# Hybrid conv, latent-attention and memory block: sums of the high and low parts of x, written by adding transfers instead of GpSimd

## The chip, the cores and the metric

The kernel runs on one core of one Trainium2 chip. A core has five engines that each work through their own list of instructions in order: TensorE (PE, matrix products), VectorE (DVE), ScalarE (ACT), GpSimd (POOL) and SyncE (SP, which here only issues transfers). They meet through semaphores. Transfers can be issued from SP, ScalarE and GpSimd, and are carried out by 16 DMA engines which all of them share. The metric is the time of one execution on the device in microseconds (us); the profile's times count from the start of its span.

## The reference

One layer of a streaming encoder, on 512 tokens of width 2048, in float32. The normalised input `h` goes through one wide input projection, whose columns feed three branches: a gated convolution, latent attention with 16 heads, and cross attention to 256 memory tokens. Each branch is gated, projected to 2048, weighted by a sigmoid gate, summed, and projected once more:

```python
h = rms_norm(x, norm_g[l])
proj = h @ w_in[l]
...
o_conv = (conv_y * jax.nn.silu(conv_z)) @ w_conv_out[l]
o_mla = (mla_y * jax.nn.silu(mla_z)) @ w_mla_out[l]
o_mem = (mem_y * jax.nn.silu(mem_z)) @ w_mem_out[l]
merged = sigmoid(g_conv) * o_conv + sigmoid(g_mla) * o_mla + sigmoid(g_mem) * o_mem
x = x + merged @ w_o[l]
```

## The kernel before

**Three products for one.** TensorE multiplies float32r operands. Each operand is split into a high part (ScalarE rounds it: `act.activation(hi, src, AF.Copy)`, L123) and a low part, the rest (VectorE: `src - hi`, L125), and a product is made of three matmuls, high x high, high x low and low x high (`mm3`, L154 to L156).

**The normalised input.** `h` is held transposed, as 16 tiles of 128 features x (high, low) x 512 tokens. Early on, SP writes them to a buffer in device memory, `hdram[k]` (shape 128 x 2 x 512, index 0 the high part, 1 the low part; L455), and reads them back after the attention (L693) into the tiles `xt[k]`: `blk` for k below 8, `hU` above.

**The planner.** From there on all the work of TensorE is a list of chunks, `plan`, and `drive()` writes the instructions of all engines chunk by chunk. For each chunk it writes, in this order: hooks that hang on this chunk number (`at[c]`, mostly loads of weights on SP), the combination of weights that a coming chunk needs (`pre`), the split of the weights of a chunk some numbers ahead (`prep`, ScalarE's high part `whi` and VectorE's low part `wlo`), small pieces that are due (`todo`, ordered by their due chunk), pieces that may run when there is room (`spare`), and then the matmuls of the chunk itself (`mm`). Nothing reorders an engine's list after that: SP's order is the written order for the whole kernel (`tc.manual_schedule`, L116), and that of the four others for this stage (L1481). A wait in such a list holds everything written behind it on the same engine.

**Two kinds of chunks.** Chunks 0 to 23 are plain: four blocks of 128 output columns, two blocks of 128 features, matmuls with 512 columns. Chunks 16 to 23 are the second half of the gate of the memory branch (`w_memz[1]`). The weights of a plain chunk are loaded by SP four chunks ahead (L852) into `raw`, a tile with four buffers. From chunk 24 on, the work comes in block groups (`block_group`), where a 2 x 2 block product is made with seven products in place of eight (`PRODUCTS`: P1, P7, P5, P6, P2, P4, P3, two chunks each, matmuls with 256 columns). The first group is the first of `w_conv`; it loads eight tiles of weights, w0 to w7 (L903), two each at chunks 21, 22, 23 and 24. Some products take sums or differences of these tiles: for P7, chunk 26 needs `s` = w0 - w2 and chunk 27 `s` = w1 - w3 (L968, VectorE), and the ones after that work in the same way in place (L973).

**The forms of x.** The block products also need sums and differences of the blocks of `h`. The tokens are halved, and feature tile p (0 to 7) is paired with tile p + 8. For each p, `x_forms(p)` has three pieces:

- `blocks` (L1212): a tile `eo` with the two whole values, high + low, of `xt[p]` and of `xt[p + 8]`. GpSimd adds them (L1215, L1216), 128 x 512 each. `eo` has the tag `r0` for even p and `r1` for odd p, each with one buffer; the tile for p + 2 takes the place of that for p.
- `sums` (L1219, with `sums_of`, L1015 to L1019): four VectorE operations make the differences and sums of the halves. L1015 reads both halves of `eo` first, L1019 reads it last.
- `parts_` (L1229): these are split into high and low parts, `f`, by ScalarE and VectorE (L123, L125).

A fourth piece, `place_t1`, splits one of the differences into the place of half of `xt[p]`.

`blocks` of p = 0 and 1 are written at chunk 15, that of p + 2 at chunk 16 + p, `sums` and `parts_` of p at chunk 17 + p (the planner gives these numbers from its own costs; pieces due at once, like `blocks`, come ahead of the spare ones, like `sums`). So `blocks` of p + 2 is written ahead of the `sums` of p that it must wait for, which are in another engine's list. The four `y` tiles that the memory gate is multiplied with (L1052, from `mydram`) are loaded at chunk 22, ahead of w2 and w3.

Of the kernel before, what the change touches and what calls it, by code (L numbers as in the profile page):

```python
# [22 lines left out]
ALU = mybir.AluOpType  # L23
# [49 lines left out]
def r32(ap):  # L73
    return ap.bitcast(F32)
# [21 lines left out]
def body(ctx, tc, a, out):  # L96
    nc = tc.nc
    act, vec, pool = nc.scalar, nc.vector, nc.gpsimd
# [177 lines left out]
    hdram = dram.tile([KB, P, 2, S], F32, name="hdram")  # L276
# [38 lines left out]
    for grp in range(4):  # L315
# [12 lines left out]
        if grp < 2:  # L328
# [12 lines left out]
            for f2 in range(2):  # L341
                b = bank("aux")
                for ff in range(2):
                    for i in range(2):
                        f = 2 * f2 + ff
                        nc.tensor.transpose(out=b[:, ff * M + i * P:ff * M + (i + 1) * P],
                                            in_=krow[i][:, f * P:(f + 1) * P], identity=ident)
# [336 lines left out]
    xt = {}  # L684
# [144 lines left out]
    def raw_b(dtype=F32):  # L829
        return psw.tile([P, KC, 512], dtype, tag="raw", name="raw", bufs=6)  # L830
# [170 lines left out]
    def operands(b0, b1, f):  # L1001
        return {"00": (b0[:, 0, :HS], b0[:, 1, :HS]), "T1": (b0[:, 0, HS:], b0[:, 1, HS:]),
                "10": (b1[:, 0, :HS], b1[:, 1, :HS]), "11": (b1[:, 0, HS:], b1[:, 1, HS:]),
                "T3": (f[:, 0, 0], f[:, 1, 0]), "T2": (f[:, 0, 1], f[:, 1, 1]), "T4": (f[:, 0, 2], f[:, 1, 2])}
# [3 lines left out]
    def f_tile(p):  # L1008
        return pf.tile([P, 2, 3, HS], F32R, name=f"f{p}")

    def sums_of(e, o, t1, then=lambda: None):

        t = pres.tile([P, S], F32, tag="u", name="t32")
        t4 = pres.tile([P, HS], F32, tag="v", name="t4", bufs=1)
        vec.tensor_tensor(out=t[:, :HS], in0=o[:, HS:], in1=e[:, HS:], op=ALU.subtract)  # L1015
        vec.tensor_tensor(out=t1, in0=e[:, HS:], in1=e[:, :HS], op=ALU.subtract)
        vec.tensor_tensor(out=t[:, HS:], in0=t[:, :HS], in1=e[:, :HS], op=ALU.add)
        then()
        vec.tensor_tensor(out=t4, in0=o[:, :HS], in1=t[:, HS:], op=ALU.subtract)  # L1019
        return t, t4  # L1020

    def split_sums(t, t4, f):
        split(pair(t), f[:, 0, :2], f[:, 1, :2])
        split(t4, f[:, 0, 2], f[:, 1, 2])
# [183 lines left out]
    def x_forms(p):  # L1208

        hold = {}  # L1210

        def blocks():  # L1212
            he, ho = xt[p], xt[p + 8]
            eo = pres.tile([P, 2, S], F32, tag=f"r{p % 2}", name="eo")
            pool.tensor_tensor(out=eo[:, 0], in0=r32(he[:, 0]), in1=r32(he[:, 1]), op=ALU.add)  # L1215
            pool.tensor_tensor(out=eo[:, 1], in0=r32(ho[:, 0]), in1=r32(ho[:, 1]), op=ALU.add)  # L1216
            hold["eo"] = eo

        def sums():  # L1219
            f = f_tile(p)  # L1220
            tx[p] = operands(xt[p], xt[p + 8], f)
            if p % 4 == 0:
                t1s["tile"] = raw_b()
            t1 = t1s["tile"].rearrange("p k n -> p (k n)")[:, (p % 4) * HS:(p % 4 + 1) * HS]
            t1s[p] = t1
            hold["t"] = sums_of(hold["eo"][:, 0], hold["eo"][:, 1], t1)
            hold["f"] = f

        def parts_():  # L1229
            split_sums(*hold["t"], hold["f"])  # L1230
        return blocks, sums, parts_
# [340 lines left out]
```

## Time and profile before

| what | value |
|---|---|
| time, median of 3 runs (lowest to highest) | 2219.71 us (2219.61 to 2223.3) |
| the profiled execution: its own time; its span | 2221.29 us; 2219.5 us |
| mean granted TensorE clock in it | 0.99 of full |
| GpSimd additions L1215, L1216 | 8 and 8, from 657.5 to 732.5 us |
| chunks 20 to 23 on TensorE | about 711.4 to 734.0 us |
| chunks 24 and 25; 26 and 27 | 734.1 to 739.8 us; 742.7 to 751.8 us |
| transfers over the span | 313.77 MB, mean 141 GB/s |

Rows of the profile read like this. In a timeline a row has the start, the duration, the engine (SPq stands for SP issuing transfers), the line, the operation, the tile written and the tiles read, shapes, and a count; rows of one kind that follow each other are merged, and the duration then runs from the first start to the last end. In brackets stands the engine's idle time ahead of the row and what ended it. In a list of waits a row has the waiting instruction, the one that released it, the total in us, how often, and the longest. In a list by line a row has min / median / max of the duration in ns, and the first and last start; a row on landing has the us from a transfer's issue to its landing, min / median / max, of the transfers that the row above it counts.

### The profile page before, as it was taken

To read this page: it belongs to the slowest core of one execution; us is meant where nothing else is said; L and a number is where in the kernel's file an instruction comes from. 1 tells how busy PE (TensorE), PEld (TensorE's weight loads), DVE (VectorE), ACT (ScalarE), POOL (GpSimd) and SP (SyncE) were. 2 spreads that over 40 slices of the span, in tenths; PEclk is the share of its full clock that TensorE was granted. 3 is DMA by queue.
4 is the path that set the end of the run, shared out by engine and by line. 5 is a ranking of instruction groups with operands and counts; after the bars stand their busy time and mean duration, and the time that the engine had idled before them with its cause. 6 is when DMAs were issued, how large, how long until landed. Compare 5 with 4: busy or idle time off the path is not lost.

```text
span 2219.5 us, 37222 instructions
## 1 busy us (share of the span) xinstructions
PE 2156.8 (97%) x15128; PEld 2019.9 (91%) x15128; DVE 1592.1 (72%) x2202; ACT 1025.3 (46%) x1547; POOL 193.6 (9%) x157
## 2 busy tenths in 40 slices
PE   7999999999999999999999999999999999997999
PEld 5788888888778899999999999999999899986999
DVE  7863777773336888787877777677776788867876
ACT  5532677764333444444444444444444444433343
POOL 7410311120012100000000000000000000012000
PEclk9999999999999999999999999999999999998999
DMA  7583212244225333333344434343245656465342
GB/s 258 155 258 101 85 58 70 69 148 147 76 76 189 115 105 100 138 102 115 124 174 171 134 115 153 115 152 134 97 145 170 244 205 200 157 237 190 115 171 86
DMA packets 110363, 313.77 MB, mean 141 GB/s; under 512 B 12656, under 2 KB 12912, under 8 KB 110192
## 3 DMA queue, kind: packets, MB, share of 16 engines
q1 hardware_dynamic: 87984, 271.20, 36.7%
q10 hardware_dynamic: 21888, 39.15, 4.7%
q8 instruction: 118, 1.93, 0.4%
q0 software_dynamic: 320, 1.05, 0.1%
q14 instruction: 53, 0.43, 0.1%
HBM read 263.12 MB, written 48.23 MB: 140 GB/s over the span
## 4 chain that ended last, share of the span: by engine, by line
PE 90%; DVE 5%; ACT 3%; issue 2%; POOL 1%; DMA 0%; SPq 0%; ACTq 0%; DVEq 0%; POOLq 0%
PE acc L154 17%; PE acc L155 17%; PE acc L156 16%; PE aux L155 12%; PE aux L156 12%; PE aux L154 12%; DVE wlo L148 1%; PE aux L205 1%; PE aux L661 1%; DVE wlo L125 1%; POOL xs L305 0%; DVE f L125 0%; DVE ml L127 0%; DVE hT L127 0%; PE aux L641 0%
## 5 line engine op out<-in xcount | busy, mean ns | idle before, releaser
L125 DVE TENSOR_TENSOR wlo<-raw,whi 128x1024 fp32r<-128x1024 f32 x440 | 539.8, 1228 | 375.9 <-ACT whi L123 375.6
L123 ACT ACTIVATE whi<-raw 128x1024 fp32r<-128x1024 f32 x440 | 465.9, 1060 | 710.0 <-PE acc L155 329.6
L973 DVE TENSOR_TENSOR raw<-raw 128x1024 f32<-128x1024 f32 x192 | 234.1, 1219 | 1.3
L154 PE MATMUL acc<-f,whi 128*128 128x256 f32 x768 | 216.8, 282 | 2.8 <-ACT whi L123 2.8
L156 PE MATMUL acc<-f,wlo 128*128 128x256 f32 x768 | 217.3, 283 | 1.6 <-DVE wlo L125 1.6
L155 PE MATMUL acc<-f,whi 128*128 128x256 f32 x768 | 216.9, 282 | 0.0
L156 PE MATMUL aux<-f,wlo 128*128 128x256 f32 x768 | 216.9, 282 | 0.0
L155 PE MATMUL aux<-f,whi 128*128 128x256 f32 x768 | 216.8, 282 | 0.0
L154 PE MATMUL aux<-f,whi 128*128 128x256 f32 x768 | 216.6, 282 | 0.0
L154 PE MATMUL acc<-blk,whi 128*128 128x256 f32 (+1 forms) x608 | 184.3, 303 | 7.0 <-ACT sq L1069 7.0
L148 DVE TENSOR_TENSOR wlo<-raw,whi 128x1024 fp32r<-128x1024 f32 (+3 forms) x97 | 117.8, 1216 | 96.6 <-ACT whi L147 95.4
L155 PE MATMUL acc<-blk,whi 128*128 128x256 f32 (+1 forms) x608 | 183.7, 302 | 0.0
L156 PE MATMUL acc<-blk,wlo 128*128 128x256 f32 (+1 forms) x608 | 183.2, 302 | 0.0
L155 PE MATMUL acc<-hU,whi 128*128 128x256 f32 (+1 forms) x608 | 182.1, 300 | 0.0
L154 PE MATMUL acc<-hU,whi 128*128 128x256 f32 (+1 forms) x608 | 182.1, 300 | 0.0
L156 PE MATMUL acc<-hU,wlo 128*128 128x256 f32 (+1 forms) x608 | 181.9, 300 | 0.0
L154 PE MATMUL aux<-blk,whi 128*128 128x256 f32 (+1 forms) x544 | 158.2, 291 | 14.4 <-ACT blk L123 12.9
L156 PE MATMUL aux<-blk,wlo 128*128 128x256 f32 (+1 forms) x544 | 158.3, 291 | 1.5 <-DVE wlo L125 1.5
L155 PE MATMUL aux<-blk,whi 128*128 128x256 f32 (+1 forms) x544 | 158.3, 291 | 0.4
L156 PE MATMUL aux<-hU,wlo 128*128 128x256 f32 (+1 forms) x544 | 156.9, 289 | 0.0
L155 PE MATMUL aux<-hU,whi 128*128 128x256 f32 (+1 forms) x544 | 156.9, 288 | 0.0
L154 PE MATMUL aux<-hU,whi 128*128 128x256 f32 (+1 forms) x544 | 156.7, 288 | 0.0
(354 smaller groups left out, 5642.0 us busy)
## 6 DMA issues: line engine op xcount, KB each, us to landing
raw<-in_w_conv SPq DMA_DIRECT2D x64, 512.0 KB, 4.4
raw<-in_w_mlaz SPq DMA_DIRECT2D x32, 512.0 KB, 5.1
raw<-in_w_gmem SPq DMA_DIRECT2D x32, 512.0 KB, 4.6
raw<-in_w_gconv SPq DMA_DIRECT2D x32, 512.0 KB, 4.8
raw<-in_w_gmla SPq DMA_DIRECT2D x32, 512.0 KB, 4.4
raw<-in_w_mla_out SPq DMA_DIRECT2D x32, 512.0 KB, 5.7
raw<-in_w_o SPq DMA_DIRECT2D x32, 512.0 KB, 6.3
raw<-in_w_mem_kv SPq DMA_DIRECT2D x31, 512.0 KB, 3.7
```

Source lines behind the costliest of these rows:

```text
L123: act.activation(hi, src, AF.Copy, scale=1.0 if g is None else g)
L125: vec.tensor_tensor(out=lo, in0=src, in1=r32(hi), op=ALU.subtract)
L148: vec.tensor_tensor(out=lo[:, cols], in0=raw[:, cols], in1=r32(hi[:, cols]), op=ALU.subtract)
L154: nc.tensor.matmul(o, lhsT=s[0], rhs=m[0], start=start, stop=False, skip_group_check=shared)
L155: nc.tensor.matmul(o, lhsT=s[0], rhs=m[1], start=False, stop=False, skip_group_check=shared)
L156: nc.tensor.matmul(o, lhsT=s[1], rhs=m[0], start=False, stop=stop, skip_group_check=shared)
L205: nc.tensor.transpose(out=b[:, i * P:(i + 1) * P], in_=s, identity=ident)
L661: nc.tensor.transpose(out=b[:, i * P:(i + 1) * P], in_=ps[i][:, j * P:(j + 1) * P], identity=ident)
L973: vec.tensor_tensor(out=w01, in0=i0, in1=i1, op=op)
```

## The change

GpSimd's additions in `blocks` are replaced by transfers. For each of the two halves of `eo`, SP loads the high part from `hdram` into `eo`, and GpSimd issues a second transfer that reads the low part from `hdram` and adds it to what stands in `eo` while writing. The second must wait until the first has landed. `xt` is no longer read here; `hdram` holds the same values. The place in the written order, the tags and the buffers stay as they were.

```diff
         def blocks():
-            he, ho = xt[p], xt[p + 8]
             eo = pres.tile([P, 2, S], F32, tag=f"r{p % 2}", name="eo")
-            pool.tensor_tensor(out=eo[:, 0], in0=r32(he[:, 0]), in1=r32(he[:, 1]), op=ALU.add)
-            pool.tensor_tensor(out=eo[:, 1], in0=r32(ho[:, 0]), in1=r32(ho[:, 1]), op=ALU.add)
+            for i in range(2):
+                nc.sync.dma_start(eo[:, i], hdram[p + 8 * i][:, 0])
+                nc.gpsimd.dma_start(out=eo[:, i], in_=hdram[p + 8 * i][:, 1], accum_op=ALU.add)
             hold["eo"] = eo
```

## The prediction

> **What bounds the kernel now.** I read the page first, then TensorE's waits around the change, then each engine in order of time there.
>
> ```profile
> PE 2156.8 (97%) x15128; PEld 2019.9 (91%) x15128; DVE 1592.1 (72%) x2202; ACT 1025.3 (46%) x1547; POOL 193.6 (9%) x157
> PE 90%; DVE 5%; ACT 3%; issue 2%; POOL 1%; DMA 0%; SPq 0%; ACTq 0%; DVEq 0%; POOLq 0%
> ...
> PE acc L154 <- ACT whi L123: 2.8, 1, 2.8
> PE acc L156 <- DVE wlo L125: 1.6, 1, 1.6
> ...
> 739.64 0.28 PE L156 MATMUL acc<-blk,wlo 128*128 128x256 f32 x1
> 742.72 0.38 PE L154 MATMUL acc<-f,whi 128*128 128x256 f32 x1 [2.81 <-ACT whi L123]
> 744.86 0.58 PE L156 MATMUL acc<-f,wlo 128*128 128x256 f32 x1 [1.64 <-DVE wlo L125]
> 751.78 0.28 PE L154 MATMUL acc<-blk,whi 128*128 128x256 f32 x1
> 744.00:746.00 2.00, 1.14 (x5) 1.14 (x6) 2.00 (x3) 0.84 (x1) 0.00 (x0) 0.62 0.63 225
> 746.00:748.00 2.00, 2.00 (x12) 2.00 (x12) 2.00 (x3) 1.34 (x2) 0.00 (x0) 0.52 0.00 0
> 748.00:750.00 2.00, 2.00 (x19) 2.00 (x18) 2.00 (x3) 1.13 (x2) 0.00 (x0) 1.00 0.00 0
> ```
>
> TensorE is the bound. Between 640 and 830 us it waits twice, both at the start of planner chunk 26 (product P7, first half). In the three windows of 2 us the granted clock stands behind the five engines' busy times: 0.62 and 0.52 after the stall, then 1.00 again. At full clock a 256-column matmul starts every 0.119 us (a chunk of 24 takes 2.9), so the 48 of chunks 26 and 27 need 5.7 us; they took from 739.76 to 751.78, 12.0. **The stall with its slow clock costs 6.3 us**, all that this region has to give.
>
> Why chunk 26 is late: VectorE.
>
> ```profile
> L125 DVE TENSOR_TENSOR f<-t,f 128x512 fp32r<-128x512 f32 (+1 forms) x12 | 19.1, 1627 | 1.4 <-ACT f L123 1.4
> ...
> 719.98 1.21 DVE L125 TENSOR_TENSOR wlo<-raw,whi 128x1024 fp32r<-128x1024 f32 x1
> 721.12 0.41 DVE L1015 TENSOR_TENSOR t<-eo 128x256 f32<-128x256 f32 x1
> 722.24 0.43 DVE L1019 TENSOR_TENSOR t<-eo,t 128x256 f32<-128x256 f32 x1
> 733.38 1.21 DVE L968 TENSOR_TENSOR s<-raw 128x1024 f32<-128x1024 f32 x1
> 734.52 1.21 DVE L125 TENSOR_TENSOR wlo<-raw,whi 128x1024 fp32r<-128x1024 f32 x1
> 737.44 1.03 DVE L125 TENSOR_TENSOR f<-t,f 128x512 fp32r<-128x512 f32 x2 [0.24 <-ACT f L123]
> 743.59 1.22 DVE L125 TENSOR_TENSOR wlo<-s,whi 128x1024 fp32r<-128x1024 f32 x1
> ...
> L1215 POOL TENSOR_TENSOR eo<-blk x8: 1283/1295/1337, 657.5 to 729.5; 128x512 f32<-128x512 f32 x8
> L1216 POOL TENSOR_TENSOR eo<-hU x8: 1299/1742/1750, 658.7 to 730.8; 128x512 f32<-128x512 f32 x8
> ```
>
> While GpSimd adds, the two `f` splits of a pair take 2 x 1.63 = 3.2 us; from 737.44, with GpSimd idle, they take 1.03. Six of the eight pairs pay 2.1 us. From 733.38 (the weight difference `s`, chunk 26's `pre`) to 744.81 (its low part) VectorE runs all but without a gap: 11.4 us.
>
> **Removed:** 16 GpSimd additions, some 24 us of POOL (8 x 1.30 + 8 x about 1.7), off TensorE's path, and with them 6 x 2.1 = 12.8 us of VectorE.
>
> **Added:** 16 plain loads of 256 KB on SP, and 16 accumulating loads on GpSimd, each behind the landing of its plain load. Each pair's loads also inherit the wait that the additions had: `eo` has one buffer for even pairs (`r0`), one for odd (`r1`), so pair p+2 waits until VectorE has done the sums of pair p (L1019). On GpSimd nothing was queued behind that wait. **On SP the weights are queued behind it.** SP keeps its written order, and the planner puts the work thus (a chunk is the line; SP's loads, then VectorE's forms):
>
> - chunk 16: weights of chunk 20, pair 2
> - chunk 17: weights of 21, pair 3; sums 0
> - chunk 18: weights of 22, pair 4; sums 1
> - chunk 19: weights of 23, pair 5; sums 2
> - chunk 20: pair 6; sums 3
> - chunk 21: w0, w1 of the first block group, pair 7; sums 4
> - chunk 22: four `y` tiles, w2, w3; low part of w0 (chunk 24), sums 5
> - chunk 23: w4, w5; `s` = w0 - w2 (chunk 26), low part of w1 (chunk 25), sums 6
> - chunk 24: sums 7, then chunk 26's low part
>
> So w0 sits behind pair 6, which waits for sums 4; and w2 sits behind pair 7, which waits for sums 5, which in VectorE's order stand behind w0's low part. Before, SP ran far ahead:
>
> ```profile
> 711.67 1.06 ACT L123 ACTIVATE whi<-raw 128x1024 fp32r<-128x1024 f32 x1 [0.52 <-ACT f L123]
> 717.27 1.06 ACT L123 ACTIVATE whi<-raw 128x1024 fp32r<-128x1024 f32 x1
> 723.69 1.04 ACT L123 ACTIVATE whi<-raw 128x1024 fp32r<-128x1024 f32 x1
> 703.18 6.34 SPq L903 DMA_DIRECT2D raw<-in_w_conv  x2
> 709.62 1.80 SPq L1052 DMA_DIRECT2D y<-mydram  x4
> 711.47 10.56 SPq L903 DMA_DIRECT2D raw<-in_w_conv  x6
> L852 SPq DMA_DIRECT2D raw<-in_w_memz x7: 327/328/333, 665.1 to 697.2; - x7
> DMA to landing us min/median/max: 3.6/3.7/4.6
> L903 SPq DMA_DIRECT2D raw<-in_w_conv x1: 430/430/430, 711.5 to 711.5; - x1
> DMA to landing us min/median/max: 7.5/7.5/7.5
> L903 SPq DMA_DIRECT2D raw<-in_w_conv x2: 430/430/430, 711.5 to 711.9; - x2
> DMA to landing us min/median/max: 7.5/7.9/8.3
> L903 SPq DMA_DIRECT2D raw<-in_w_conv x4: 328/430/1030, 711.5 to 715.2; - x4
> DMA to landing us min/median/max: 7.5/7.9/9.1
> ```
>
> The third and fourth rows from above are ScalarE's split of w0 and SP's issue of w0 and w1; the landing rows are w2 alone, w2 with w3, and w2 to w5. w0 went out at 703.2, w2 at 711.5, far ahead of their use at 723.7 and 733.4. The new chain, step by step:
>
> 1. Weights of chunks 21 to 23 now go out behind sums 0, 1, 2 plus two `eo` issues of 0.45 (the `y` row's 1.80 / 4). ScalarE splits chunk 22 at 711.67 and chunk 23 at 717.27, one chunk of TensorE apart (5.6); so chunk 21 at 706.07. Its low part starts at 707.1, sums 2 follow 1.14 later and take 1.55 (719.98, 721.12, 722.67 before): done at 709.8. Chunk 23's weights go out at 710.7 and land by 715.3 at the longest landing, 4.6. Hidden, with 2 us of room.
> 2. Low part of chunk 23 at 717.27 + 1.06 = 718.4 (before 719.98, with VectorE behind). Sums 4 follow and are done 2.7 later, at 721.1.
> 3. Pair 6 goes out at 721.1 and 721.55, w0 at 722.0. Landing 4.5 (the upper end, since 512 KB go ahead): 726.5, against 703.2 + 3.6 = 706.8 before.
> 4. ScalarE 1.06, low part 1.14, sums 5 1.55: 730.2. TensorE needs w0 at 734.0 (739.76 less two chunks of 2.9), so no stall yet.
> 5. Pair 7 from 730.2, four `y` from 731.1, w2 at 732.9, the seventh issue.
> 6. Landing of w2. The same burst without the pair ran before: first `y` at 709.62, w2 landed at 711.47 + 7.5 = 719.0, 9.35 later. A pair adds 512 KB ahead; in that burst neighbours of 512 KB landed about 1.25 apart (711.9 + 8.3 = 720.2 behind 719.0). So 730.2 + 9.35 + 1.25 = **740.8**. At the shortest landing, 3.6, it would be 736.5.
> 7. VectorE stands at `s` until then, and the low part of chunk 25 (734.52 before) stands behind it. TensorE finishes chunk 24 near 737 and waits for that low part until 743, then from about 746 to 752 for chunk 26. From `s` on VectorE's chain is the old one of 11.4 us, since GpSimd was idle through it before too (its last addition, 730.8 plus 1.7, ends at 732.5).
>
> **The sum:** chunk 26 moves by the shift of `s`, 740.8 - 733.4 = **+7.5 us** (+3.1 at the shortest landing). The old 6.3 us are not saved: the 11.4 us chain comes back whole, and the slow clock with it, as TensorE again idles some 5 us before. Behind it TensorE has no other wait up to 830, so the shift stays to the end. The 12.8 us that VectorE saves become waiting for w0 and w2. The profiled execution takes 2221.29 us (span 2219.5, 1.8 around it), inside the runs' 2219.61 to 2223.3; it would become 2228.8, and the median of 2219.71 becomes **2227.2**.
>
> **The unknown price: an accumulating load.** No row shows one. The nearest are GpSimd's plain stores of the same size, and a lone plain `eo` pair later:
>
> ```profile
> L678 POOL DMA_DIRECT2D ydram<-y x4: 539/544/753, 495.9 to 536.9; - x4
> DMA to landing us min/median/max: 2.3/2.5/5.0
> L1391 SPq DMA_DIRECT2D eo<-adram x2: 327/472/618, 1741.4 to 1741.8; - x2
> DMA to landing us min/median/max: 2.5/3.0/3.4
> ```
>
> Call it A, from GpSimd's issue to landing. One turn of a buffer is sums 1.55, second issue 0.48, landing 3.4, A: 5.4 + A, against two chunks of TensorE, 11.2. Up to A = 5.8 it hides behind the chunks; above, sums 4 come 2 x (A - 5.8) later after two turns, and so do w0, w2 and `s`. Lower end 2.3. Upper end 12: the crowded store's 5.0, twice for reading source and destination, and 2 for queueing beside the weights. I take 5, the crowded store, at which nothing is added; it costs +12.4 at the upper end.
>
> The Trainium skill (SBUF — State Buffer, "SBUF: two separate sides") says that GpSimd cannot write a transfer's descriptors while VectorE runs an operation that uses both port pairs. All VectorE rows quoted here are TENSOR_TENSOR, which the page ("Who interferes with whom") exempts, so by it A gains nothing; if they did lock, one 1.2 us operation for each of two issues would add up to 2.4 a turn, and A = 5 would then cost some 3 us over two turns. No row here can show it. The skill (DMA: Bandwidth & Descriptors, "Rules for kernel authors") also asks that an accumulating transfer wait for the earlier write's semaphore; without that wait the landing of 3.4 would leave the turn. No row shows either.
>
> **Rivals.**
>
> *Faster: VectorE's relief reaches TensorE.* Place: chunk 26. For it: `f` at 3.2 against 1.03 us beside GpSimd. Price: at most the 6.3 us, 2213.4. It decides from the point where w2 lands before 733.4; that needs it issued by 729.8, hence sums 5 done by 727.2, three us before step 4, or SP not held by the waits. Against: SP's four `y` loads at 709.62 went out only behind w1 (703.18 plus 6.34 ends at 709.5), so SP is in order.
>
> *Small loss.* The burst drains as a lone load does: +3.1, 2222.8. For it: 3.6 to 4.6 us landings of single loads. Against: 7.5 in the only like burst.
>
> *Slow accumulation paces the forms.* With A = 10: 7.5 + 8.4 = +15.9, 2235.6. For it: reading and rewriting the destination. Against: only 256 KB each, on a queue that is otherwise empty.
>
> *The change does not do what it says* (the transfers wait nowhere new, level): only if `eo` were free early; its buffers are not, L1019 reads them last.
>
> **How the numbers follow.** Three runs before spread over 0.17%, so 0.2%, 4.4 us, is what a measurement can tell. Forecast 55%, slow accumulation 22%, small loss 15%, faster 6%, level 2%. Slower takes the first two and a little of the small loss: 0.78. Same: the rest of that and level, 0.16. Faster 0.06. Range: from the small loss less the stretch of its steps, 2222, to A = 12, 7.5 + 12.4 = +19.9, 2239.6: it leaves out the faster case and the tails. The forecast alone spans +4.4 to +10, by the landing of w2 between 738 and 743.
>
> **What would show it.** Right: SP's `raw<-in_w_conv` w0 near 722 and w2 near 733, held by `DVE t L1019`; VectorE idle before `s` L968, released by a load; `f` near 1.0 us throughout; TensorE idle near 737 to 743 and again before chunk 26; that chunk at about 750. Wrong: w2 out before 729 (faster), sums 2 and 4 waiting for GpSimd's transfers (slow accumulation), or a stall of chunks 21 to 23, whose 2 us of room step 1 counts on. Wrong as a whole: TensorE's wait in 730 to 760 no longer than before.

## The result, and the profile after

The changed kernel takes 2233.4 us (median of 5, 2232.03 to 2245.25), the kernel before 2220.52 (median of 5, 2219.61 to 2223.3): a ratio of 1.0057, 95% interval 1.0029 to 1.0084, **slower by some 13 us**. 2227.2 had been predicted, 7.5 us above the runs known then, with a range of 2222.0 to 2239.6. The profiled execution took 2233.24 us with a span of 2231.4, 11.9 us longer than that of before.

Executions of most kernels here, the one before included (14 of 76 beside the experiments), fall into two groups some 10 us apart, for a reason that no trace here shows; where that shifts a median, the median of the lower group stands beside it.

Two clocks must be set against each other first. SP's `y` loads ahead of its first `eo` load (one row before, one after) show that the profiled execution after runs 2.0 us early when it comes to the changed stage:

```profile
672.48 1.80 SPq L1052 DMA_DIRECT2D y<-mydram  x4
```

```profile
670.50 1.80 SPq L1052 DMA_DIRECT2D y<-mydram  x4
```

So 2.0 is taken off each time that was predicted before it is compared. Some 1.5 of it stood before the change could act (VectorE's L1107 starts at 642.82 before and 641.33 after). The other 0.5 is a small gain of the change that the prediction did not have: before, the additions of pairs 0 and 1 run from 657.45 on, VectorE's L1116 beside them takes 1.81 us in place of 0.62, and eight of TensorE's matmuls (L205) that read what L1116 writes take 1.54 us in place of 1.03.

The page of after, busy time and share of each engine:

```profile
PE 2160.4 (97%) x15128; PEld 2022.4 (91%) x15128; DVE 1579.7 (71%) x2202; ACT 1025.5 (46%) x1547; POOL 185.1 (8%) x157
```

VectorE is busy 12.4 us less than before (1592.1), which is the relief that was forecast. TensorE around the block products: first every wait that it has between 640 and 850 us, in order of time, then two windows of 2 us with the granted clock (the third figure from the right).

```profile
733.56 0.39 PE L154 MATMUL acc<-blk,whi 128*128 128x256 f32 x1 [1.31 <-ACT whi L123]
734.82 0.39 PE L156 MATMUL acc<-blk,wlo 128*128 128x256 f32 x1 [0.76 <-DVE wlo L125]
...
747.76 0.58 PE L156 MATMUL acc<-blk,wlo 128*128 128x256 f32 x1 [8.34 <-DVE wlo L125]
...
754.69 0.39 PE L154 MATMUL acc<-f,whi 128*128 128x256 f32 x1 [1.86 <-ACT whi L123]
756.83 0.58 PE L156 MATMUL acc<-f,wlo 128*128 128x256 f32 x1 [1.64 <-DVE wlo L125]
```

```profile
748.00:750.00 2.00, 2.00 (x10) 2.00 (x11) 1.73 (x5) 1.26 (x4) 0.00 (x0) 0.50 1.08 338
...
758.00:760.00 2.00, 2.00 (x12) 2.00 (x11) 2.00 (x3) 1.38 (x2) 0.00 (x0) 0.54 0.00 0
```

The two waits of before (2.8 and 1.6 us, at chunk 26) are still there as 1.86 and 1.64. New is the wait of 8.34 us for the low part of chunk 25, and two small ones at chunk 24. Chunk 26 begins at 754.69 against 742.72, 12.0 us later. The clock stands at 0.50 after the long wait and once more near 0.54 after chunk 26's.

Why that low part was late. VectorE in order of time, SP likewise, and one row of SP's waits between 660 and 800 us:

```profile
696.21 0.43 DVE L1019 TENSOR_TENSOR t<-eo,t 128x256 f32<-128x256 f32 x1
...
708.97 0.42 DVE L1019 TENSOR_TENSOR t<-eo,t 128x256 f32<-128x256 f32 x1
...
723.27 0.42 DVE L1019 TENSOR_TENSOR t<-eo,t 128x256 f32<-128x256 f32 x1
723.93 1.03 DVE L125 TENSOR_TENSOR f<-t,f 128x512 fp32r<-128x512 f32 x2 [0.24 <-ACT f L123]
733.54 1.23 DVE L125 TENSOR_TENSOR wlo<-raw,whi 128x1024 fp32r<-128x1024 f32 x1 [7.91 <-ACT whi L123]
735.80 0.43 DVE L1019 TENSOR_TENSOR t<-eo,t 128x256 f32<-128x256 f32 x1
745.35 1.23 DVE L968 TENSOR_TENSOR s<-raw 128x1024 f32<-128x1024 f32 x1 [7.18 <-DMA raw<-in_w_conv]
755.56 1.22 DVE L125 TENSOR_TENSOR wlo<-s,whi 128x1024 fp32r<-128x1024 f32 x1
```

```profile
696.66 0.80 SPq L1215 DMA_DIRECT2D eo<-hdram  x2
709.42 1.25 SPq L1215 DMA_DIRECT2D eo<-hdram  x2
718.16 6.38 SPq L1215 DMA_DIRECT2D eo<-hdram  x4
724.64 0.89 SPq L903 DMA_DIRECT2D raw<-in_w_conv  x2
736.26 0.80 SPq L1215 DMA_DIRECT2D eo<-hdram  x2
737.11 1.85 SPq L1052 DMA_DIRECT2D y<-mydram  x4
739.06 47.41 SPq L903 DMA_DIRECT2D raw<-in_w_conv  x16
```

```profile
SPq L1215 <- DVE t L1019: 18.3, 6, 5.3
```

The first three rows are the ends of sums 0, 2 and 4. Sums 4 end at 723.69 (L1019 at 723.27 and 0.42); then SP issues pair 6, and w0 and w1 at 724.64. Sums 5 end at 736.23; SP issues pair 7 at 736.26, the four `y` tiles, and w2 at 739.06. VectorE idles 7.91 us until w0 is split and 7.18 until w2 has landed. This is the chain that was forecast, link by link, only later. `f` takes 1.03 us.

How long the loads took, in the list by line (a row on landing under the transfers that it counts: SP's plain loads of `eo`, GpSimd's adding ones, and w0 with w1; w0 is the 7.7):

```profile
L1215 SPq DMA_DIRECT2D eo<-hdram x16: 319/423/942, 678.8 to 736.6; - x16
DMA to landing us min/median/max: 2.8/5.0/7.0
L1216 POOL DMA_DIRECT2D eo<-hdram x16: 872/876/1883, 684.4 to 740.2; - x16
DMA to landing us min/median/max: 3.8/6.3/10.1
L903 SPq DMA_DIRECT2D raw<-in_w_conv x2: 385/397/409, 724.6 to 725.2; - x2
DMA to landing us min/median/max: 7.7/8.4/9.1
```

w2, issued at 739.06, landed 6.3 us later, when `s` starts.

### The profile page after: what moved, and what is told of

It reads as the page before. It is cut to its first block, busy times and chain, and to the rows that moved or that the text cites. A ratio compares the mean times of both kernels' runs of the same rounds, so it can differ in the third digit from the quotient of the medians.

```text
span 2231.4 us, 37263 instructions
## 1 busy us (share of the span) xinstructions
PE 2160.4 (97%) x15128; PEld 2022.4 (91%) x15128; DVE 1579.7 (71%) x2202; ACT 1025.5 (46%) x1547; POOL 185.1 (8%) x157
## 4 chain that ended last, share of the span: by engine, by line
PE 89%; DVE 4%; ACT 2%; DMA 2%; issue 1%; POOL 1%; SPq 0%; ACTq 0%; DVEq 0%; POOLq 0%
PE acc L154 16%; PE acc L155 16%; PE acc L156 16%; PE aux L155 12%; PE aux L154 12%; PE aux L156 12%; DVE wlo L148 1%; DMA eo<-hdram 1%; PE aux L205 1%; PE aux L661 1%; DMA raw<-in_w_conv 1%; POOL xs L305 0%; DVE hT L127 0%; PE aux L641 0%; PE aux L642 0%
## 5 line engine op out<-in xcount | busy, mean ns | idle before, releaser
L154 PE MATMUL aux<-blk,whi 128*128 128x256 f32 (+1 forms) x544 | 158.2, 291 | 14.5 <-ACT blk L123 12.9
```

The costliest lines, as they stand in the source:

```text
L154: nc.tensor.matmul(o, lhsT=s[0], rhs=m[0], start=start, stop=False, skip_group_check=shared)
```

## Experiments

Three theories stood at the start. **Theory 1**, the forecast: weights stand in SP's list behind plain loads that wait for sums. **Theory 2**: the adding transfers are slow and pace the forms. **Theory 3**: the added traffic as such. Each edit is shown against the changed kernel unless it says otherwise; a run's "before" was timed beside it (medians: 2220.24 us of 24 for the first three runs and the first timing of four buffers, 2221.38 of 28 for its second timing and the runs with moved `y` loads, 2220.65 of 24 for the others).

**No adding transfer, SP as changed.** GpSimd adds the low part with an instruction:

```diff
-                nc.gpsimd.dma_start(out=eo[:, i], in_=hdram[p + 8 * i][:, 1], accum_op=ALU.add)
+                pool.tensor_tensor(out=eo[:, i], in0=eo[:, i], in1=r32(xt[p + 8 * i][:, 1]), op=ALU.add)
```

> SP loads the high parts into eo exactly where the changed kernel does, but GpSimd then adds the low part with an addition (eo + low part of xt), so no transfer accumulates. Theory 1 (the weights stand in SP's list behind loads that wait for the sums): w0 and w2 go out late all the same, near 722 and 733 us, and the time is 5 to 9 us above before, some 2225 to 2229. Theory 2 (the accumulating transfers are slow and pace the sums): with none left the loss goes, 2218 to 2222.

Measured: 2232.04 us (6 runs), ratio 1.0041 (1.0023 to 1.0060). SP's issue of w2, in order of time, and VectorE's wait for it:

```profile
735.70 48.11 SPq L903 DMA_DIRECT2D raw<-in_w_conv  x16
```

```profile
DVE s L968 <- DMA raw<-in_w_conv: 6.6, 1, 6.6
```

Nearly the whole loss, 11.8 us (more than the 5 to 9 of Theory 1), without one adding transfer and with half the added traffic. Theory 2 as worded falls, and Theory 3 loses most of its ground. The forms come late in this run too, for another reason: beside GpSimd's additions VectorE's sums take longer (sums 2 run from 706.04 to 709.78, 3.7 us against 1.55 in the changed kernel).

**Adding transfer kept, SP as before.** GpSimd copies the high part, then issues the adding transfer:

```diff
-                nc.sync.dma_start(eo[:, i], hdram[p + 8 * i][:, 0])
+                pool.tensor_copy(eo[:, i], r32(xt[p + 8 * i][:, 0]))
```

> GpSimd copies the high part from xt into eo and issues the accumulating transfer behind it; SP's list is that of the kernel before. Theory 1: weights go out as early as before (w0 near 702, w2 near 711), no stall of 8 us before chunk 25; time within -4 to +3 us of before. Theory 2: sums 2 to 7 still wait for the accumulating transfers, turn after turn, and the time is 9 to 13 us above before, like the changed kernel.

Measured: 2220.79 us (12 runs), ratio 1.0013 (0.9996 to 1.0030); lower group 2220.36, that of before 2219.95. SP's issue of w0 and w2 in order of time:

```profile
702.52 5.93 SPq L903 DMA_DIRECT2D raw<-in_w_conv  x2
711.22 83.19 SPq L903 DMA_DIRECT2D raw<-in_w_conv  x18
```

The weights go out as early as before, TensorE waits as before (2.9 us for `whi`, before 2.8), and no loss is left that the runs can tell. These two runs each have one landing in a turn of a buffer, from the issue of a pair's loads to its sums. The run that has it in SP's list loses 11.8 us, the run that has it in GpSimd's list 0.4 (between the lower groups). That points to the list that holds the wait.

**The second transfer overwrites** (the sums then lack the high part of `h`), all else as changed:

```diff
-                nc.gpsimd.dma_start(out=eo[:, i], in_=hdram[p + 8 * i][:, 1], accum_op=ALU.add)
+                nc.gpsimd.dma_start(out=eo[:, i], in_=hdram[p + 8 * i][:, 1])
```

> As the changed kernel, but GpSimd's second transfer overwrites instead of adding: the sums lack the high part here, all instructions stay. It prices the adding itself. Theory 1: landing from GpSimd's issue falls from 5 to 7 us to 3 to 5, sums come 1 to 2 us earlier a turn, but w0 and w2 stay behind them: 5 to 9 us above before. Theory 2: most of the loss goes, at most 4 us above before.

Measured: 2236.01 us (6 runs, the lower three 2229.63 to 2231.26), ratio 1.0063 (1.0039 to 1.0087). The price of adding, by the same rows as those of after above:

```profile
L1216 POOL DMA_DIRECT2D eo<-hdram x16: 546/546/608, 685.3 to 736.1; - x16
DMA to landing us min/median/max: 2.9/4.8/7.5
```

By the medians adding costs 0.33 us more to issue and 1.5 us more to land, but most of the loss is there without it: 11.3 us between the lower groups (2231.26 against 2219.95), again more than the 5 to 9 of Theory 1, where the change lost 12.7 (2233.24, the median of its lower three, against 2220.52). The forms do come earlier. The end of sums 4:

```profile
720.93 0.42 DVE L1019 TENSOR_TENSOR t<-eo,t 128x256 f32<-128x256 f32 x1
```

This execution is 1.1 us early (first sums at 695.92, before's at 697.06), so sums 4 end at 722.5 of before's clock. Before had 722.67, and the changed kernel has 725.7 by the same reckoning: in these two executions adding makes the forms some 3 us late. Even so `s` starts at 743.13, 10.9 us later than before, since w2, issued at 735.25, takes 7.9 us to land.

**Pairs 6 and 7 by GpSimd's additions, 0 to 5 as changed**, which frees w0 and w2 of the last two pairs:

```diff
+            if p >= 6:
+                for i, h in enumerate((xt[p], xt[p + 8])):
+                    pool.tensor_tensor(out=eo[:, i], in0=r32(h[:, 0]), in1=r32(h[:, 1]), op=ALU.add)
+            else:
                 for i in range(2):
...
```

> Pairs 0 to 5 as in the changed kernel, pairs 6 and 7 added by GpSimd as before, so that SyncE's list holds nothing for them and the weights w0 and w2 stand behind the loads of pair 5 alone (they wait for the sums of pair 3). Theory 1 (weights behind loads that wait for sums): w0 is issued near 718 (changed kernel: 724.6) and w2 near 721 (739.1), VectorE no longer waits more than 1 us for w2, TensorE's stall at the 26th chunk falls back to about that of before, and the time to 0 to 3 us above before. Theory 2 (slow accumulating transfers pace the forms): six of the eight pairs still come by them, so at least 8 of the 12 us of loss stay.

Measured: 2227.97 us (12 runs), ratio 1.0037 (1.0021 to 1.0054); lower group 2225.95 against 2220.40, **+5.5**. SP in order of time, TensorE's longest waits, and VectorE in order of time:

```profile
718.87 1.16 SPq L903 DMA_DIRECT2D raw<-in_w_conv  x2
722.21 76.83 SPq L903 DMA_DIRECT2D raw<-in_w_conv  x18
```

```profile
PE acc L156 <- DVE wlo L125: 5.3, 2, 3.7
```

```profile
732.41 0.43 DVE L1015 TENSOR_TENSOR t<-eo 128x256 f32<-128x256 f32 x1 [4.33 <-DMA eo<-hdram]
737.90 1.21 DVE L968 TENSOR_TENSOR s<-raw 128x1024 f32<-128x1024 f32 x1
```

The weights went out as Theory 1 said, and `s` no longer waits for w2. Yet only about half of the loss came back, so **Theory 1 alone (0 to 3 us) is too small**, and the 8 or more of Theory 2 too large. The rest is in the first VectorE row: sums 5 wait 4.33 us for their transfers, and `s` stands behind them in VectorE's list. By then this execution is 1.2 us early (its first sums begin at 695.90, before's at 697.06); so sums 5 begin 5.8 us later than before's 727.82, and `s` 5.7 later than its 733.38. That is the run's +5.5. The forms have a pace of their own: the second adding load of pair 5 went out at 722.8 and took 9.5 us to land, beside the weights issued from 718.87 on.

**The other half: pairs 0 to 5 by GpSimd, only 6 and 7 by the transfers:**

```diff
+            if p < 6:
+                for i, h in enumerate((xt[p], xt[p + 8])):
+                    pool.tensor_tensor(out=eo[:, i], in0=r32(h[:, 0]), in1=r32(h[:, 1]), op=ALU.add)
+            else:
                 for i in range(2):
...
```

> The other half: pairs 0 to 5 added by GpSimd as before, only pairs 6 and 7 by the transfers, so that w0 stands behind pair 6's loads and w2 behind pair 7's. Theory 1: w0 is issued at 720 to 723, w2 at 730 to 735, VectorE waits 5 us or more for w2, and most of the loss is there with a quarter of the transfers: 7 to 12 us above before. Theory 2: a quarter of the transfers gives at most a quarter of the loss, 0 to 3 us. Theory 3 (the added traffic as such): likewise 0 to 3 us.

Measured: 2230.57 us (6 runs), ratio 1.0043 (1.0028 to 1.0058). SP and VectorE in order of time:

```profile
727.02 0.85 SPq L903 DMA_DIRECT2D raw<-in_w_conv  x2
739.25 48.36 SPq L903 DMA_DIRECT2D raw<-in_w_conv  x16
```

```profile
745.74 1.22 DVE L968 TENSOR_TENSOR s<-raw 128x1024 f32<-128x1024 f32 x1 [7.41 <-DMA raw<-in_w_conv]
```

This execution is 3.3 us late when the forms begin (700.38 against 697.06), so w0 is at 723.7 and w2 at 735.9 of before's clock, 0.7 and 0.9 us past what was expected. **A quarter of the transfers makes +10** (lower groups 2230.51 and 2220.40): with no late forms ahead of it, the place in SP's list does that alone. Theory 3 is done with.

**The plain loads two chunks later**, so that w0 to w5 stand, two at a time, ahead of pairs 5, 6 and 7 in SP's list:

```diff
-            later(0, 0, xf[p + 2][0])
+            later(2, 0, xf[p + 2][0])
```

> The changed kernel with each pair's transfers written two chunks later, so that w0 and w1 stand ahead of pair 5's loads and w2 and w3 ahead of pair 6's. Theory 1: w0 is issued near 712, w2 by 722, the wait for w2 is gone, and the time is 0 to 4 us above before; what is late next are pairs 6 and 7 themselves, whose forms TensorE wants from about 755 on. Theory 2 (the pace of the transfers): the forms come later still, so the time is as in the changed kernel or worse, 12 us or more above before.

Measured: 2231.40 us (5 runs), ratio 1.0046 (1.0029 to 1.0063). SP, TensorE and VectorE, each in order of time:

```profile
712.60 0.84 SPq L903 DMA_DIRECT2D raw<-in_w_conv  x2
...
718.94 0.96 SPq L903 DMA_DIRECT2D raw<-in_w_conv  x2
```

```profile
750.96 0.58 PE L154 MATMUL acc<-f,whi 128*128 128x256 f32 x1 [10.95 <-ACT whi L123]
```

```profile
734.73 1.22 DVE L968 TENSOR_TENSOR s<-raw 128x1024 f32<-128x1024 f32 x1
...
747.29 0.42 DVE L1015 TENSOR_TENSOR t<-eo 128x256 f32<-128x256 f32 x1 [3.06 <-DMA eo<-hdram]
```

The weights are early, `s` starts at 734.73, and TensorE waits 10.95 us all the same: for chunk 26's weights, split behind the sums of pair 7, which now come at 747.29. Theory 1's 0 to 4 us was wrong here too; the 10.8 lost are nearer to the 12 or more of Theory 2. Moving the loads back freed one chain and put the delay on the other.

**Four buffers for `eo`** in place of two (pairs 2, 3, 6 and 7 in tiles that were free by then), transfers as changed:

```diff
-            eo = pres.tile([P, 2, S], F32, tag=f"r{p % 2}", name="eo")
+            if p in (2, 3):
+                eo = psw.tile([P, KC, 512], F32, tag="s3", name="eo", bufs=2)
+            elif p in (6, 7):
+                eo = raw_b()
+            else:
+                eo = pres.tile([P, 2, S], F32, tag=f"r{p % 2}", name="eo")
```

> The changed kernel with eo in more buffers: pairs 2 and 3 in the two tiles that P7's weight difference takes later, pairs 6 and 7 in two of the free weight tiles. Loads of eo then hardly wait for sums, on SP or GpSimd, and the transfers start 10 us earlier. Theory 1: w0 goes out near 702 and w2 near 715 again, VectorE keeps the 12 us that GpSimd's additions took, the stall before chunk 26 goes: 4 to 6 us below before, 2214 to 2217. Theory 2 expects the same, since an early start hides a slow transfer. If the added 8 MB of traffic were the cause (theory 3), it stays above before, 2223 to 2233.

Measured: 2218.23 us (11 runs), ratio 0.9986 (0.9969 to 1.0003). The same kernel, timed a second time:

> The four-buffer kernel once more, beside the one with the y loads moved, on the same chip: 2216 to 2220 undisturbed, 1 to 4 us below before, as at its first timing (0.9986 of before, interval 0.9969 to 1.0003).

2218.19 us (12 runs), ratio 0.9988 (0.9972 to 1.0003). Of the first, GpSimd's adding loads by line with their landing, SP's issue of w2 in order of time, and TensorE's only two waits of over 1 us in the stage:

```profile
L1221 POOL DMA_DIRECT2D eo<-hdram x12: 872/875/1877, 683.4 to 710.6; - x12
L1221 POOL DMA_DIRECT2D raw<-hdram x4: 872/874/875, 712.4 to 723.7; - x4
DMA to landing us min/median/max: 6.7/7.9/10.5
```

```profile
716.65 72.79 SPq L903 DMA_DIRECT2D raw<-in_w_conv  x18
```

```profile
PE acc L154 <- ACT whi L123: 1.8, 1, 1.8
PE acc L156 <- DVE wlo L125: 1.6, 1, 1.6
```

All the transfers are there, their landings are longer than in the changed kernel, and the loss is gone. w2 goes out at 716.65 in place of 739.06, and VectorE's list of waits has none for a transfer of `eo`. So neither the transfers nor adding as such cost time; **two buffers did**. With them a pair's loads wait for the sums two pairs back, and that wait both holds the weights behind it in SP's list and stretches the turn of the forms. The run lifts both at once and does not tell them apart; the two runs that divide the pairs do. Of the 4 to 6 us of gain expected, 2 were measured, not clear of noise: TensorE still waits 3.4 us for chunk 26, as VectorE waits 3.8 us for w2.

**GpSimd's additions in the same four buffers** (the same edit on the kernel before):

> GpSimd's additions as before, with the results of pairs 2, 3, 6 and 7 in buffers of their own, as in the run that had the transfers in four buffers and came out at 0.9986 of before. No addition waits for the sums two pairs back any more; the weights stand as before. If that run gained by the buffers, this one gains too: 1 to 5 us below before, with the same 3.2 us for the slowed f operations. If it gained by taking the additions off GpSimd, this one is within 1 us of before.

Measured: 2218.68 us (11 runs), ratio 0.9994 (0.9978 to 1.0010). It does not tell what it was to tell: its interval holds both no change and the four-buffer kernel's gain.

**The `y` loads out of w2's way**: four buffers, and the second group's four `y` loads issued by GpSimd, with the transfers and with the additions:

```diff
-    def y_tile(src):
+    def y_tile(src, queue=None):
         t = pres.tile([P, S], F32, tag="y", name="y", bufs=4)
-        nc.sync.dma_start(t, src)
+        (queue or nc.sync).dma_start(out=t, in_=src)
...
-... ys.append(y_tile(mydram[4 * grp + i])))
+... ys.append(y_tile(mydram[4 * grp + i], nc.gpsimd if grp else None)))
```

> The kernel with the transfers in four buffers, and the four y loads of the second memory group moved from SyncE's list to GpSimd's, so that w2 stands right behind w1. Theory: in the four-buffer kernel the pairs came every 5.6 us and what was left was VectorE's wait of 3.8 us for w2, which stood behind the y loads. Expected: w2 issued by 711 instead of 716.65, that wait under 1 us, TensorE's 3.4 us before the 26th chunk down to 2 us or less, and 1 to 3 us below the four-buffer kernel of the same call: 2215 to 2217. The other reading, that the 3.4 us are ScalarE's and VectorE's own time for the first weights of that group: no change, within 0.5 us.

> GpSimd's additions in four buffers, with the same move of the y loads. If the transfers themselves gain by sparing VectorE the slow f operations (3.2 us against 1.03), this one stays 1 to 3 us above the kernel with transfers, four buffers and moved y loads; if only the buffers and the place of the weights count, the two are within 1 us.

Measured: 2224.08 us (12 runs), ratio 1.0003 (0.9988 to 1.0018), and 2228.43 us (12 runs), ratio 1.0012 (0.9994 to 1.0030). In the first, w2 goes out at 709.80, `s` no longer waits, and TensorE's waits in the stage shrink to one of 1.1 us, as expected; but only 3 of its 12 executions took 2212.07 to 2214.73 us, and 9 took 2222.4 to 2226.2. With the additions 5 took 2218.15 to 2220.83 and 7 took 2228.38 to 2230.97. So neither is a gain that can be relied on, and whether the transfers gain by sparing VectorE the slow `f` stays open. No kernel here is shown to beat the one before: the four-buffer kernel's two intervals each just reach 1.

## Why the prediction was right, and what was mis-sized

The sign, the place and the main mechanism held: TensorE waits at chunk 25, VectorE waits for w2 at `s`, and w2 stands in SP's list behind a pair that waits for sums 5. The size did not: the 12.9 us measured lie above the +4.4 to +10 that the forecast alone spans, and only the upper end, set by the rival "slow accumulation", takes them in. Step by step, with 2.0 us taken off what was predicted:

| step | predicted | measured |
|---|---|---|
| sums 2 done | 707.8 | 709.4 |
| sums 4 done | 719.1 | 723.7 |
| w0 issued; landing | 720.0; 4.5 | 724.6; 7.7 |
| sums 5 done | 728.2 | 736.2 |
| w2 issued; landing | 730.9; 7.9 | 739.1; 6.3 |
| `s` | 738.8 | 745.35 |
| from `s` to the end of chunk 26's low part | 11.4 | 11.4 |
| shift of `s` against before | +7.5 | +14.0 |

(740.8 - 733.4 is 7.4; the prediction wrote 7.5.) The shift of 14.0 less the 2.0 us that this execution was ahead is its 11.9 us of loss, but for 0.1. Since 0.5 of the 2.0 is the change's own gain, the trace puts the change at some 13.5 us; the medians say 12.9.

**The removed work** was right: 12.8 us of VectorE were to go, 12.4 went, and `f` takes 1.03 us for all pairs. In this stage it bought nothing, as said; it became waiting for w0 and w2.

**Step 1** (chunks 21 to 23 hidden with 2 us of room) held: TensorE has no wait there, although sums 2 came 1.6 us late.

**The turn of a buffer** is the term that was mis-sized most. It was put at 10.4 us against 11.2 of cover, so no delay. The turn from sums 0 to sums 2 took 12.75 (696.64 to 709.39), that to sums 4 14.3 (to 723.69), so step 2 came 4.6 us late. In the first, GpSimd's second adding load went out 1.1 us behind its first (701.45 and 700.36), where the sum had 0.48 for a second issue, and landed in 6.3 us instead of 5. In the second, SP issued at 709.42, and the second adding load went out 7.6 us later:

```profile
717.06 0.88 POOL L1216 DMA_DIRECT2D eo<-hdram  x1 [0.65 <-DMA eo<-hdram]
```

The plain half that it waited for had taken 7.0 us to land, not 3.4; its own landing took 5.0, as assumed. The 3.4 came from a lone pair late in the kernel, though this stage's DMA engines were to be busy with weights. The rival "slow accumulation" had this term, but looked for it in A alone. The run with overwriting transfers shows what adding has in it: without it sums 4 are on time, but most of the loss stays (11.3 of 12.7 us).

**Step 3's landing of w0** was 3.2 us too short: its 4.5, "the upper end", came from `w_memz` loads, which landed in 4.6 at most and had no pair of `eo` ahead of them. **Step 6's landing of w2** was 1.6 too long. 4.6 + 3.2 - 1.6 and some 0.3 in the steps between make the 6.5 us by which `s` missed.

**Step 4** said no stall yet at chunk 24; w0's lateness made two of 1.31 and 0.76 us.

**The slow clock** came back at chunk 26 as said. That it would also stand at 0.50 through chunk 25 was not in the sum; it cost little, as VectorE's 11.4 us from `s` on outlast it: TensorE waits 1.86 us more for chunk 26 even so.

**The rivals.** "Faster" failed at the condition that it named: SP was not let off the waits (18.3 us behind `DVE t L1019`). "Small loss" needed landings of 3.6; w2 took 6.3. "Slow accumulation" was half right: the forms did come at a slower pace, worth 5.5 us by itself (pairs 6 and 7 by GpSimd). Adding has a part in that pace, as the overwriting run shows, but a turn with the adding load alone, behind GpSimd's copy, loses nothing that can be told; the pace shows only where a plain landing stands ahead of the adding one. The forecast's own mechanism is worth 10 us by itself (only pairs 6 and 7 by the transfers). They don't add up to 15.5, since both end at the same `s`.

The Trainium skill (DMA: Bandwidth & Descriptors, "Rules for kernel authors") asks that an accumulating transfer wait for the earlier write. The kernel keeps that wait, and in the trace SP's plain landing, median 5.0 us, stands in every turn; what happens without it no run here shows. The Trainium skill (DMA: Bandwidth & Descriptors, "Anatomy of one DMA — SWDGE (gpsimd) path") also says that a semaphore wait is taken by the issuing sequencer, not by the DMA engines. The trace agrees: weights that need nothing of those sums went out at 724.64 and 739.06, behind pairs that wait for them. The Trainium skill's port rule that the prediction cites (SBUF — State Buffer, "SBUF: two separate sides") was not tested by an experiment. The trace shows no sign of a lock beside VectorE's TENSOR_TENSOR operations: the issue at 717.06, beside sums 3, took 0.875 us, as did the one at 715.54, while VectorE was idle.

## What to carry to other kernels

When work moves from an engine to a DMA queue, list what that queue holds behind each new wait: here loads of weights that need nothing of it were held for the sums of an earlier pair, and a quarter of the transfers made most of the loss. A transfer's landing in a buffer's turn has to be taken from rows of the same crowded stage, and two landings in series may need more buffers; with four the same transfers cost no time that these runs can tell. After freeing one late chain, look which one ends last next: moving the loads two chunks back fixed the weights and lost 11 us through the forms.

## What the runs showed of the hardware

An adding load of 256 KB takes GpSimd 0.876 us to issue and lands in 3.8 to 10.1 us, median 6.3; the same load without adding, at the same place, takes 0.546 us and lands in 2.9 to 7.5, median 4.8. The Trainium skill's fit for one transfer (DMA: Bandwidth & Descriptors, "Anatomy of one DMA — SWDGE (gpsimd) path": 2.0 us and its bytes at 436 GB/s) would give 2.6 us as an estimate. SP's plain loads of `eo` came that low, 2.5 us at the least in the run with the loads two chunks later, against a median of 5.0 in the changed kernel; no adding load of any run landed in less than 3.7. That the weights in flight beside them make the rest is likely, but no run separates it. With four buffers the adding loads took longer still (6.7 to 10.5, median 7.9) and cost no time. Beside GpSimd's additions some of VectorE's operations are slower: two `f` splits take 3.2 us against 1.03, the sums of a pair 3.7 against 1.55, L1116 1.81 against 0.62.
